# Feed-forward pairs, parts two and three: one product of 512 columns for both halves of an operand

## The chip, the cores and the metric

The kernel runs on one core of a Trainium2 chip. The metric is the device time of one execution in microseconds, as the median of several runs. A profile is the record of one such execution, taken by the hardware profiler. The engines are PE (the matrix engine TensorE; PEld is its weight loading), DVE (VectorE, element by element), ACT (ScalarE, copies and functions), POOL (GpSimd) and SP (SyncE, which issues transfers). Products are summed in PSUM, a small memory of eight banks, each of 512 fp32 numbers per partition; DVE and ACT read them out into SBUF, where all other tiles lie.

## The reference

The program is an encoder of two layers over 512 tokens of 1024 channels. Each layer mixes tokens by three parallel branches, then runs a gated feed-forward part and a gated input embedding. Only the feed-forward part is touched:

```python
D_FF = int(math.ceil(8 * D_MODEL / 3 / 256) * 256)   # 2816
...
h = rmsnorm(x, norm_ffn[i])
x = x + (jax.nn.silu(h @ w_ffn_gate[i]) * (h @ w_ffn_up[i])) @ w_ffn_down[i]
```

All arrays are fp32, the inputs x, p and the parameters are drawn from normal distributions, and the output is (1, 512, 1024).

## The kernel before, in words

**Precision.** PE multiplies operands of type fp32r, which keep fewer bits than fp32. So every operand is split into a high part (a rounded copy, made on ACT) and a low part (the rest, by a subtraction on DVE; `split`, line 162). A product is three matmuls added into one PSUM tile: high weight by high operand, high weight by low operand, low weight by high operand. `mm3` (lines 175 to 179) does this for most of the kernel, with 512 columns (tokens) each.

**The feed-forward part** (`ffn`, line 1094) has 22 blocks of 128 inner channels. They come in three parts of 8, 7 and 7 blocks (`PARTS`, line 40). In each part the blocks' gate and up products are made first (the *pair stage*; a *pair* is one block's gate and up weights), then the part's share of the down product is made for the eight output blocks and subtracted from x (the *down stage*).

**A pair** (`seven`, line 959) treats gate and up, and the two halves of the tokens and of the channels, as a 2 by 2 product of blocks, and makes it with seven products in place of eight (the Strassen-Winograd scheme). Weights are a11, a12, a22 and the sums s1 to s4; operands are b11, b21, b22 and the sums t1 to t4. Each product sums over four k-blocks of 128 channels and has 256 columns (half of the tokens): four times the three matmuls of lines 1004 to 1006, 84 matmuls for a pair. The operands are made once per layer in `quarters` (line 928): t1 to t4 are tiles of shape [128, 2, 256], high part and low part one behind the other; b11, b21 and b22 are cut out of the tiles h, [128, 2, 512], in which the high part's 512 columns lie ahead of the low part's.

**The running sums.** Partial sums live in the PSUM tiles C, A, Q (three banks, of the tags mm for even blocks and sc, sc, av for odd ones) and T (tag tr). They hold 256 columns each, half of a bank. In parts two and three the steps of a pair, each ended by a `yield`, are:

1. C = a11·b11; ACT copies C into A.
2. T = s1·t3; ACT copies T into uu[:, 0].
3. A += s3·t2; ACT copies A into Q; the gate of the pair before is started (`flush`: Silu on ACT, multiply on DVE, then the split into the down product's operand); C += a12·b21 (`corner`), and DVE writes C times the row factor rb into gg[:, 0].
4. A += s2·t1; ACT copies A into uu[:, 1]; Q += a22·t4; DVE adds uu[:, 0] to uu[:, 1] and Q to uu[:, 0].
5. A += s4·b22; DVE writes A times rb into gg[:, 1].

**The order of the work.** PE's order is the program's. `sevens_of` (line 1058) weaves two pairs: step 1 of the next, 4 of this one, 2 of the next, 5 of this one, 3 of the next; the last pair of a part runs its steps 4 and 5 alone. The other engines' orders are set by the compiler's scheduler from priorities; weight loading and splitting are put up to 400 instructions ahead (line 963). Each engine then works strictly through its own queue, waiting at an instruction until what that one needs is there. A pair's weights need, on ACT and DVE, two splits of 1024 columns (a11 with a12, s1 with s2), one of 512 (a22), two additions on DVE (s3, s4) and a third split of 1024 columns (s3 with s4, into tiles of tags pt or y). The sums s1 and s2 are formed by transfers that POOL issues (line 974).

The first block of part one has a variant of its own (`early`), which the change leaves as it is.

Of the kernel before, what the change touches and what calls it, by code (L numbers as in the profile page):

```python
# [12 lines left out]
F32R = mybir.dt.float32r  # L13
I32 = mybir.dt.int32
AF = mybir.ActivationFunctionType
ALU = mybir.AluOpType
# [4 lines left out]
P = 128  # L21
# [40 lines left out]
class Net:  # L62
# [211 lines left out]
    def norm_chunk(self, k, x, g, tag, st, n=512):  # L274

        if k == KD - 1:
            self.sumsq(k, x, st)
        if n < 512:
            tag = tuple(a[:, :n] for a in self.halves(self.sb(tag, [P, 2, 512], F32R)))
        h = self.operand(x[:, :n], g, tag)  # L280
        if k < KD - 1:
            self.sumsq(k, x, st)
        return h
# [644 lines left out]
    def quarters(self, x, h, j):  # L928


        one, two = slice(0, 256), slice(256, 512)
        g = lambda k: self.par(self.i, "ffn", k)
        f = []
        for k in (2 * j, 2 * j + 1):
            v = self.sb("t", [P, 512])
            self.act(v, x[k], AF.Copy, scale=g(k))
            f.append(v)
        b11, b12, b21, b22 = f[0][:, one], f[0][:, two], f[1][:, one], f[1][:, two]
        u = self.sb("t", [P, 2, 256])
        w = self.sb("t", [P, 2, 256])  # L940
        t1, t2, t3, t4 = u[:, 0], u[:, 1], w[:, 0], w[:, 1]
        self.tt(t1, b11, b12, ALU.subtract)
        self.stt(t2, t1, -1.0, b22, ALU.mult, ALU.subtract)
        self.tt(t3, b22, b12, ALU.subtract)
        self.stt(t4, t2, -1.0, b21, ALU.mult, ALU.subtract)
        if j < 2:
            d = [self.sb("rp", [P, 2, 256], F32R) for _ in range(2)]
            d += [self.sb("b", [P, 2, 256], F32R) for _ in range(2)] if j else \
                self.parts_of("v", [2, 256], 2, F32R)
        else:  # L950
            d = [q for n in range(2) for q in self.zs[2 * j - 4 + n]]
        for o, t in zip(d, (t1, t2, t3, t4)):
            self.held = self.split(o[:, 0], o[:, 1], t)
        ha, hb = self.halves(h[2 * j]), self.halves(h[2 * j + 1])
        cut = lambda p, c: (p[0][:, c], p[1][:, c])
        return dict(b11=cut(ha, one), b21=cut(hb, one), b22=cut(hb, two),
                    **{f"t{n + 1}": (o[:, 0], o[:, 1]) for n, o in enumerate(d)})

    def seven(self, wg, wu, bs, tags, spare, md, first, fb, early):


        nc = self.nc
        with self.tc.high_priority(offset=min(self.w_ahead, self.tc.cur_priority - self.p0)):
            lo, up = slice(0, 512), slice(512, 1024)
            g, a22 = self.sb("wr", [P, 1024]), self.sb("r", [P, 512])
            sums = self.sums[self.sevens % 3], self.sums[3]
            self.sevens += 1
            s1, s2, s3, s4 = (s[:, q:q + 512] for s in sums for q in (0, 512))
            nc.sync.dma_start(s1, wg[:, lo])
            nc.sync.dma_start(s2, wu[:, up])  # L970
            nc.sync.dma_start(g, wg)
            nc.sync.dma_start(a22, wu[:, up])
            for q in (s1, s2):
                nc.gpsimd.dma_start(q, wu[:, lo], accum_op=ALU.add)  # L974
            ws = {}

            def halve(hi, lo, src, names):
                i = self.split(hi, lo, src)
                for q, name in enumerate(names):
                    c = slice(q * 512, q * 512 + 512)  # L980
                    ws[name] = (hi[:, c], lo[:, c])
                return i

            wide = lambda: (self.sb("wh", [P, 1024], F32R), self.sb("wl", [P, 1024], F32R))
            i = halve(*wide(), g, ("a11", "a12"))
            if fb == 1:
                self.behind(i, self.held)
            low = halve(self.sb("kh", [P, 512], F32R), self.sb("a", [P, 512], F32R), a22, ("a22",))
            halve(*wide(), sums[0], ("s1", "s2"))
            i = self.tt(s3, s1, a22, ALU.add)  # L990
            self.behind(i, low)
            if first or fb < 3:
                self.behind(i, self.held if fb else self.mark)
            self.tt(s4, s3, g[:, up], ALU.add)
            halve(*spare, sums[1], ("s3", "s4"))
        C, A, Q = (self.ps(t, (P, 256)) for t in tags)

        def product(out, w, b, first=False):
            wh, wl = ws[w]
            mm = nc.tensor.matmul  # L1000
            for k in range(4):
                c = slice(k * P, k * P + P)
                bh, bl = bs[k][b]
                mm(out, wh[:, c], bh, start=first and k == 0, stop=False, skip_group_check=True)  # L1004
                mm(out, wh[:, c], bl, start=False, stop=False, skip_group_check=True)  # L1005
                mm(out, wl[:, c], bh, start=False, stop=k == 3, skip_group_check=True)  # L1006
            self.chunk2()

        gg, uu = self.sb("t", [P, 2, 256]), self.sb("t", [P, 2, 256])
        def corner():  # L1010
            product(C, "a12", "b21")
            if not early:
                self.tt(gg[:, 0], C, self.halved(0), ALU.mult)

        product(C, "a11", "b11", True)
        self.act(A, C, AF.Copy)
        yield
        if early:
            Z = self.ps("tr", (P, 256))
            product(Z, "s4", "b22", True)  # L1020
            self.act(gg[:, 1], Z, AF.Copy)
            corner()
            yield
        T = self.ps("tr", (P, 256))
        product(T, "s1", "t3", True)
        self.act(uu[:, 0], T, AF.Copy)
        yield
        product(A, "s3", "t2")
        self.flush(self.act(Q, A, AF.Copy))
        if not early:  # L1030
            corner()
        yield
        product(A, "s2", "t1")
        self.act(uu[:, 1], A, AF.Copy)
        product(Q, "a22", "t4")
        self.tt(uu[:, 1], uu[:, 1], uu[:, 0], ALU.add)
        self.tt(uu[:, 0], Q, uu[:, 0], ALU.add)
        if early:
            self.tt(gg[:, 0], C, self.halved(0), ALU.mult)
            self.tt(gg[:, 1], A, gg[:, 1], ALU.add)  # L1040
        yield
        if not early:
            product(A, "s4", "b22")
        self.tt(gg[:, 1], gg[:, 1] if early else A, self.halved(1), ALU.mult)

        def rest(then):
            i = self.act(gg, gg, AF.Silu, table="silu")
            if then is not None:
                self.behind(i, then)
            self.tt(gg, gg, uu, ALU.mult)  # L1050
            self.held = self.split(*self.halves(md), gg.rearrange("p a b -> p (a b)"))

        self.pending.append(rest)
# [40 lines left out]
    def ffn(self, h, x):  # L1094
# [3 lines left out]
        st, hn, bs = [], [], self.four  # L1098
# [4 lines left out]
        for part in PARTS:  # L1103
            mids = md8[:len(part)]
            self.sevens_of((self.seven(self.a["w_fg"][i, fb], self.a["w_fu"][i, fb], bs,
                                       (("mm", "mm", "mm"), ("sc", "sc", "av"))[fb % 2],
                                       spare[fb % 2], md8[f], part[0] and f < 2, fb, fb == 0)
                            for f, fb in enumerate(part)), part[0] == 0)
            self.flush()
            down = [self.a["w_fd"][i, m][:, part[0] * P:(part[-1] + 1) * P] for m in range(KD)]  # L1110
            two = [self.ps(("mm", "sc")[part[-1] % 2 == 0]) for _ in range(2)]
            self.pair(two, down[:2], mids)
            for m in range(KD):
                if m < 2:
                    ps = two[m]
                else:
                    ps = self.ps("mm")
                    self.gemm(ps, down[m], mids)
                d = self.sb("t", [P, 512])
                self.tt(d, ps, self.rb, ALU.mult)  # L1120
                self.tt(x[m], x[m], d, ALU.subtract)
                if part is PARTS[-1]:
                    if m in (0, 2):
                        qk = self.parts_of("qk", [2, 512], 2, F32R)
                    hn.append(self.norm_chunk(m, x[m], self.par(i, "ple", m),
                                              qk[m % 2] if m < 4 else "z", st))
# [350 lines left out]
```

## Time and profile before

| | |
|---|---|
| median of 3 runs | 1771.03 us (1770.5 to 1771.51) |
| the profiled execution | 1770.93 us |
| its span, first to last instruction | 1769.2 us |
| granted TensorE clock | 0.999 of full |
| pair stages of parts two and three, both layers | 617.2 to 687.6, 725.7 to 796.1, 1493.7 to 1564.1, 1602.2 to 1672.5 us |

The profile's page gives busy time per engine and, as its fourth part, the chain of work that ended last: followed back from the last instruction, at each step to what released it. The windows view gives, for a stretch of the span, its length and each engine's busy time in it, with the number of instructions in brackets. The timeline has one row for each instruction: its start, its duration, its engine, the line of the kernel that issued it, the tile written and the tiles read, the shape; in square brackets stands how long the engine was idle before it and what ended that. Lines 143 and 157 are the helpers through which nearly all of ACT's and DVE's work goes, so their rows are told apart by their tiles: ffn_wh and ffn_wl are high and low weights, ffn_wr, ffn_r and ffn_qk raw ones and their sums, ffn_t the gates' tiles uu and gg, ffn_mm, ffn_sc, ffn_av and ffn_tr PSUM tiles by tag, wo_rb the row factor.

A matmul's duration reaches from its start until its results are written; the next one starts long before that. What a matmul costs PE is therefore the time from its start to the next one's.

### The profile page before, as it was taken

How to read it: one execution, taken by the hardware profiler on the slowest of the kernel's cores; microseconds unless marked ns; L12 is line 12 of the kernel's file. 1: busy time of each engine (PE TensorE's matmuls, PEld its weight loads, DVE VectorE, ACT ScalarE, POOL GpSimd, SP SyncE). 2: the span in 40 equal slices, each digit the busy share in tenths (PEclk: the TensorE clock that was granted, in tenths of full speed). 3: DMA queues.
4: the chain of work that ended last, by engine and by line, in shares of the span. 5: the costliest groups of instructions: out<-in, count | busy, mean ns of one | idle time of the engine just before them, and what ended most of it. 6: DMA issues, size and time to landing. Idle time of an engine off the chain costs nothing.

```text
span 1769.2 us, 27111 instructions
## 1 busy us (share of the span) xinstructions
PE 1760.0 (99%) x10146; PEld 1553.3 (88%) x10146; DVE 1361.1 (77%) x2220; ACT 900.6 (51%) x1559; POOL 104.0 (6%) x114
## 2 busy tenths in 40 slices
PE   9999999999999999999999999999999999999998
PEld 7889888888899899998888888888888998989987
DVE  7967988998787576777776789789888865866676
ACT  5566555326575254454545655552356643634444
POOL 0000000000121010100000000000001210101000
PEclk9999999999999999999999999999999999999999
DMA  6575642334767375543546655323356664655332
GB/s 229 158 191 156 169 116 56 104 104 154 208 170 183 107 172 150 143 120 125 158 128 168 193 141 163 100 76 94 103 192 177 179 168 118 173 144 155 95 104 96
DMA packets 114788, 253.95 MB, mean 144 GB/s; under 512 B 16864, under 2 KB 23776, under 8 KB 114656
## 3 DMA queue, kind: packets, MB, share of 16 engines
q1 hardware_dynamic: 101264, 227.83, 42.5%
q0 software_dynamic: 12672, 23.07, 8.1%
q8 instruction: 80, 1.31, 0.3%
q10 hardware_dynamic: 720, 1.31, 0.2%
q14 instruction: 52, 0.43, 0.1%
HBM read 215.46 MB, written 7.34 MB: 126 GB/s over the span
## 4 chain that ended last, share of the span: by engine, by line
PE 98%; DVE 1%; ACT 1%; issue 0%; POOL 0%; POOLq 0%; ACTq 0%; DVEq 0%
PE ffn_mm L177 4%; PE ffn_mm L178 4%; PE ffn_mm L179 4%; PE ffn_mm L1006 3%; PE ffn_mm L1004 3%; PE ffn_mm L1005 3%; PE ffn_sc L1004 3%; PE ffn_sc L1005 3%; PE ffn_sc L1006 3%; PE mergea_mm L177 2%; PE mergea_mm L179 2%; PE mergea_mm L178 2%; PE diff_sc L796 2%; PE diff_mm L177 2%; PE diff_mm L178 2%; PE gatec_mm L178 2%
## 5 line engine op out<-in xcount | busy, mean ns | idle before, releaser
L160 DVE SCALAR_TENSOR_TENSOR conv_z<-glu_z,pre_par,conv_z 128x512 f32<-128x512 f32 x240 | 179.6, 748 | 3.4
L143 ACT ACTIVATE ffn_wh<-ffn_wr 128x1024 fp32r<-128x1024 f32 (+1 forms) x92 | 93.3, 1021 | 141.8 <-PE ffn_mm L178 76.6
L157 DVE TENSOR_TENSOR ffn_wl<-ffn_wr,ffn_wh 128x1024 fp32r<-128x1024 f32 (+1 forms) x92 | 107.6, 1175 | 41.3 <-ACT ffn_wh L143 40.9
L974 POOL DMA_DIRECT2D ffn_qk<-w_fu x88 | 77.9, 981 | 601.6 <-DMA ffn_qk<-w_fu 288.0
L157 DVE TENSOR_TENSOR ffn_t<-ffn_mm,wo_rb 128x512 f32<-128x512 f32 (+1 forms) x86 | 47.8, 557 | 72.2 <-PE ffn_mm L179 61.9
L143 ACT ACTIVATE mergea_wh<-mergea_wr 128x1024 fp32r<-128x1024 f32 (+1 forms) x32 | 27.1, 846 | 96.8 <-PE mergea_mm L178 79.6
L157 DVE TENSOR_TENSOR ffn_wl<-ffn_qk,ffn_wh 128x1024 fp32r<-128x1024 f32 x44 | 53.9, 1224 | 15.2 <-ACT ffn_wh L143 15.2
L143 ACT ACTIVATE ffn_wh<-ffn_qk 128x1024 fp32r<-128x1024 f32 x44 | 46.6, 1059 | 33.0 <-PE ffn_mm L178 16.2
L143 ACT ACTIVATE diff_a<-diff_sc,diff_s 128x512 f32<-128x512 f32 x32 | 22.0, 688 | 71.1 <-DVE diff_s L889 71.1
L177 PE MATMUL ffn_mm<-ffn_v,ffn_wh 128*128 128x512 f32 x132 | 51.4, 389 | 0.0
L178 PE MATMUL ffn_mm<-ffn_v,ffn_wh 128*128 128x512 f32 x132 | 51.4, 389 | 0.0
L179 PE MATMUL ffn_mm<-ffn_v,ffn_wl 128*128 128x512 f32 x132 | 51.3, 389 | 0.0
L177 PE MATMUL ffn_mm<-ffn_y,ffn_wh 128*128 128x512 f32 x132 | 51.3, 389 | 0.0
L178 PE MATMUL ffn_mm<-ffn_y,ffn_wh 128*128 128x512 f32 x132 | 51.3, 389 | 0.0
L179 PE MATMUL ffn_mm<-ffn_y,ffn_wl 128*128 128x512 f32 x132 | 51.3, 389 | 0.0
L1004 PE MATMUL ffn_mm<-wo_h,ffn_wh 128*128 128x256 f32 x176 | 49.9, 284 | 0.0
L1005 PE MATMUL ffn_sc<-wo_h,ffn_wh 128*128 128x256 f32 x176 | 49.8, 283 | 0.0
L1006 PE MATMUL ffn_mm<-wo_h,ffn_wl 128*128 128x256 f32 x176 | 49.8, 283 | 0.0
L1006 PE MATMUL ffn_sc<-wo_h,ffn_wl 128*128 128x256 f32 x176 | 49.8, 283 | 0.0
L1004 PE MATMUL ffn_sc<-wo_h,ffn_wh 128*128 128x256 f32 x176 | 49.8, 283 | 0.0
L1005 PE MATMUL ffn_mm<-wo_h,ffn_wh 128*128 128x256 f32 x176 | 49.8, 283 | 0.0
L143 ACT ACTIVATE natten_wh<-natten_wr 128x1024 fp32r<-128x1024 f32 x24 | 25.4, 1058 | 42.1 <-issue 15.2
(862 smaller groups left out, 6483.4 us busy)
## 6 DMA issues: line engine op xcount, KB each, us to landing
ffn_qk<-w_fu POOLq DMA_DIRECT2D x88, 256.0 KB, 6.4
ffn_wr<-w_fg SPq DMA_DIRECT2D x44, 512.0 KB, 4.4
ffn_wr<-w_fd SPq DMA_DIRECT2D x32, 448.0 KB, 4.2
ffn_r<-w_fu SPq DMA_DIRECT2D x44, 256.0 KB, 3.2
ffn_qk<-w_fg SPq DMA_DIRECT2D x44, 256.0 KB, 3.1
ffn_qk<-w_fu SPq DMA_DIRECT2D x44, 256.0 KB, 3.3
natten_wr<-w_in SPq DMA_DIRECT2D x16, 512.0 KB, 4.4
diff_wr<-w_in SPq DMA_DIRECT2D x16, 512.0 KB, 4.2
```

The lines of the kernel that those rows point to most:

```text
L143: i = self.nc.scalar.activation(out, in_, func, **kw)
L157: return self.nc.vector.tensor_tensor(out, a, b, op)
L160: return self.nc.vector.scalar_tensor_tensor(out, a, s, b, op0, op1)
L177: mm(out, wh, ah, start=first, stop=False, **kw)
L178: mm(out, wh, al, start=False, stop=False, **kw)
L179: mm(out, wl, ah, start=False, stop=last, **kw)
L796: self.nc.tensor.matmul(out, st4[:, u, qs], keys(st), start=first and n == 0, stop=n == 1, **kw)
L974: nc.gpsimd.dma_start(q, wu[:, lo], accum_op=ALU.add)
L1004: mm(out, wh[:, c], bh, start=first and k == 0, stop=False, skip_group_check=True)
L1005: mm(out, wh[:, c], bl, start=False, stop=False, skip_group_check=True)
L1006: mm(out, wl[:, c], bh, start=False, stop=k == 3, skip_group_check=True)
```

## The change

In parts two and three (`twice`), C, A and Q get 512 columns, in two halves of 256: a full bank. A product into such a tile makes, per k-block, one matmul of the high weights with the operand's high and low parts side by side (512 columns; the sums with the high part land in the first half, those with the low part in the second), and one of the low weights with the high part (256 columns, first half). So it has two matmuls where it had three. T keeps its 256 columns and its three matmuls. The two halves are added when a tile is read out. As one DVE instruction doesn't take both halves from PSUM here, ACT copies the second half to SBUF and DVE adds the first one to it. The copies of C into A and of A into Q take both halves. T goes to gg[:, 1] and is added to both parts of uu in one broadcast addition. C is read at the end of step 5 and no longer in step 3, and both parts of gg are multiplied by rb in one instruction. Operands are handed on as [128, 2, 256] slices in place of tuples of two; part one takes its three matmuls from these slices.

```diff
@@ norm_chunk
-            tag = tuple(a[:, :n] for a in self.halves(self.sb(tag, [P, 2, 512], F32R)))
+            tag = self.sb(tag, [P, 2, 512], F32R)[:, :, :n]
@@ quarters
-        ha, hb = self.halves(h[2 * j]), self.halves(h[2 * j + 1])
-        cut = lambda p, c: (p[0][:, c], p[1][:, c])
-        return dict(b11=cut(ha, one), b21=cut(hb, one), b22=cut(hb, two),
-                    **{f"t{n + 1}": (o[:, 0], o[:, 1]) for n, o in enumerate(d)})
+        ha, hb = h[2 * j], h[2 * j + 1]
+        return dict(b11=ha, b21=hb[:, :, one], b22=hb[:, :, two],
+                    **{f"t{n + 1}": o for n, o in enumerate(d)})
@@ seven
-        C, A, Q = (self.ps(t, (P, 256)) for t in tags)
+        shape = (P, 2, 256) if twice else (P, 256)
+        C, A, Q = (self.ps(t, shape) for t in tags)
...
-                bh, bl = bs[k][b]
-                mm(out, wh[:, c], bh, start=first and k == 0, stop=False, skip_group_check=True)
-                mm(out, wh[:, c], bl, start=False, stop=False, skip_group_check=True)
-                mm(out, wl[:, c], bh, start=False, stop=k == 3, skip_group_check=True)
+                both = bs[k][b]
+                if len(out.shape) > 2:
+                    mm(out, wh[:, c], both, start=first and k == 0, stop=False, skip_group_check=True)
+                    mm(out[:, 0], wl[:, c], both[:, 0], start=False, stop=k == 3, skip_group_check=True)
+                    continue
+                mm(out, wh[:, c], both[:, 0], start=first and k == 0, stop=False, skip_group_check=True)
+                mm(out, wh[:, c], both[:, 1], start=False, stop=False, skip_group_check=True)
+                mm(out, wl[:, c], both[:, 0], start=False, stop=k == 3, skip_group_check=True)
@@ corner
-            if not early:
+            if not early and not twice:
                 self.tt(gg[:, 0], C, self.halved(0), ALU.mult)
@@ step 2
-        self.act(uu[:, 0], T, AF.Copy)
+        shared = gg[:, 1] if twice else uu[:, 0]
+        self.act(shared, T, AF.Copy)
@@ step 4
         product(A, "s2", "t1")
-        self.act(uu[:, 1], A, AF.Copy)
+        if twice:
+            self.act(uu[:, 1], A[:, 0], AF.Copy)
+            self.act(gg[:, 0], A[:, 1], AF.Copy)
+        else:
+            self.act(uu[:, 1], A, AF.Copy)
         product(Q, "a22", "t4")
-        self.tt(uu[:, 1], uu[:, 1], uu[:, 0], ALU.add)
-        self.tt(uu[:, 0], Q, uu[:, 0], ALU.add)
+        if twice:
+            self.tt(uu[:, 1], uu[:, 1], gg[:, 0], ALU.add)
+            self.act(uu[:, 0], Q[:, 1], AF.Copy)
+            self.tt(uu[:, 0], Q[:, 0], uu[:, 0], ALU.add)
+            self.tt(uu, uu, gg[:, 1:2].to_broadcast([P, 2, 256]), ALU.add)
+        else:
+            self.tt(uu[:, 1], uu[:, 1], uu[:, 0], ALU.add)
+            self.tt(uu[:, 0], Q, uu[:, 0], ALU.add)
@@ step 5
-        self.tt(gg[:, 1], gg[:, 1] if early else A, self.halved(1), ALU.mult)
+        if twice:
+            for n, o in enumerate((C, A)):
+                self.act(gg[:, n], o[:, 1], AF.Copy)
+                self.tt(gg[:, n], o[:, 0], gg[:, n], ALU.add)
+            self.tt(gg, gg, self.rb.rearrange("p (a b) -> p a b", a=2), ALU.mult)
+        else:
+            self.tt(gg[:, 1], gg[:, 1] if early else A, self.halved(1), ALU.mult)
```

`ffn` passes `part[0] > 0` as `twice`.

More of the change, by code (lines that the diff above doesn't have):

```diff
@@ L953, in quarters, with seven @@
             self.held = self.split(o[:, 0], o[:, 1], t)
-        ha, hb = self.halves(h[2 * j]), self.halves(h[2 * j + 1])
-        cut = lambda p, c: (p[0][:, c], p[1][:, c])
-        return dict(b11=cut(ha, one), b21=cut(hb, one), b22=cut(hb, two),
-                    **{f"t{n + 1}": (o[:, 0], o[:, 1]) for n, o in enumerate(d)})
-    def seven(self, wg, wu, bs, tags, spare, md, first, fb, early):
+        ha, hb = h[2 * j], h[2 * j + 1]
+        return dict(b11=ha, b21=hb[:, :, one], b22=hb[:, :, two],
+                    **{f"t{n + 1}": o for n, o in enumerate(d)})
+    def seven(self, wg, wu, bs, tags, spare, md, first, fb, early, twice):
         nc = self.nc
@@ L1106, in ffn @@
                                        (("mm", "mm", "mm"), ("sc", "sc", "av"))[fb % 2],
-                                       spare[fb % 2], md8[f], part[0] and f < 2, fb, fb == 0)
+                                       spare[fb % 2], md8[f], part[0] and f < 2, fb, fb == 0,
+                                       part[0] > 0)
                             for f, fb in enumerate(part)), part[0] == 0)
```

## The prediction

> **What bounds the kernel now.** I read the page first (busy times and the chain that ended last), then the stages of the feed-forward part in the windows view, then the timeline of PE, ACT and DVE inside one of them.
>
> ```profile
> span 1769.2 us, 27111 instructions
> ...
> PE 1760.0 (99%) x10146; PEld 1553.3 (88%) x10146; DVE 1361.1 (77%) x2220; ACT 900.6 (51%) x1559; POOL 104.0 (6%) x114
> ...
> PE 98%; DVE 1%; ACT 1%; issue 0%; POOL 0%; POOLq 0%; ACTq 0%; DVEq 0%
> ```
>
> PE is busy nearly without a hole and makes up 98% of the chain that ended last. So time leaves this kernel only where PE gets shorter, and it comes back wherever another engine makes PE wait. The stages that the change touches are the pairs of parts two and three in both layers:
>
> ```profile
> core 0: us, PE busy (x) PEld busy (x) DVE busy (x) ACT busy (x) POOL busy (x), PEclk, DMA share, GB/s
> 617.20:687.60 70.40, 70.40 (x589) 70.33 (x589) 51.36 (x77) 41.00 (x67) 12.38 (x14) 1.00 0.69 169
> 687.60:725.70 38.10, 38.10 (x170) 31.54 (x169) 23.87 (x33) 10.18 (x11) 0.00 (x0) 1.00 0.37 117
> 725.70:796.10 70.40, 70.40 (x590) 70.36 (x589) 50.78 (x76) 39.74 (x65) 7.03 (x8) 1.00 0.52 136
> 1493.70:1564.10 70.40, 70.40 (x590) 70.36 (x589) 51.40 (x77) 40.99 (x67) 12.37 (x14) 1.00 0.69 170
> 1602.20:1672.50 70.30, 70.30 (x589) 70.27 (x588) 50.73 (x76) 39.73 (x65) 7.08 (x8) 1.00 0.49 128
> ```
>
> The four rows of about 70.4 us are the pair stages; the 38.1 us row is a down stage, shown for its matmuls of 512 columns. In each pair stage PE is busy from end to end at full clock. Seven pairs of 84 matmuls are 588 (the count takes in one or two that straddle an edge).
>
> **What a matmul costs here.** A start-to-start time is what a matmul adds to PE, since the durations overlap. From the windows: 70.35 us / 588 = 119.6 ns for 256 columns, and 38.1 us / 168 (eight outputs of seven blocks, three each) = 226.8 ns for 512. The single rows agree, at both changes of width:
>
> ```profile
> 573.58 0.28 PE L1006 MATMUL ffn_sc<-wo_h,ffn_y 128*128 128x256 f32 x1
> 573.70 0.40 PE L177 MATMUL ffn_mm<-ffn_v,ffn_wh 128*128 128x512 f32 x1
> 573.93 0.40 PE L178 MATMUL ffn_mm<-ffn_v,ffn_wh 128*128 128x512 f32 x1
> ...
> 617.02 0.39 PE L179 MATMUL ffn_mm<-ffn_e,ffn_wl 128*128 128x512 f32 x1
> 617.25 0.28 PE L1004 MATMUL ffn_mm<-wo_h,ffn_wh 128*128 128x256 f32 x1
> ```
>
> 256 before 512 takes 0.12 us, 512 before 256 takes 0.23, so a mixed order costs each its own time. Two of 256 are 239.2 ns, one of 512 is 226.8: each merged pair saves 12.4 ns.
>
> **Change, PE.** Six of a pair's seven products are merged; the seventh, into T (s1 by t3), is not, because T stays a tile of 256 columns and the new branch asks for three dimensions. A product has four k-blocks, so 6 x 4 = 24 merges in a pair, 24 x 7 x 4 stages = 672 in all: 672 x 12.4 ns = 8.4 us less PE. A pair goes from 10.05 us (70.35 / 7) to 9.75.
>
> The Trainium skill, page "TensorE: Matmul & The Clock Gate", section "Back-to-back issue gap", speaks against most of this: it puts the fixed cost of a warm matmul at about 2.5 ns over its columns, by which 672 merges are worth about 1.7 us (an estimate from that page). The rows disagree: 2 x 119.6 - 226.8 is 12.4 ns, and they decide.
>
> **Change, layout.** The sliced tiles in place of tuples (norm_chunk, quarters) name the same bytes with the same instructions: nothing. The moving operand b11, b21 or b22 now spans two runs of 256 columns that lie apart; no row of 512 columns has that. Bounds: nothing, and the whole 12.4 ns. I take nothing, nearest to the 512-column rows.
>
> **Change, ACT and DVE, in the middle of a stage.** Per pair ACT widens two copies (A from C, Q from A) to 512 and gains four of 256 (the second halves of A, Q, C and A again). DVE keeps its four ops of 256 and gains two of 512: the broadcast add of T, and one multiply by rb over both halves in place of a part of the old ones (the old multiplies become adds). The rows:
>
> ```profile
> 681.98 0.37 ACT L143 ACTIVATE ffn_mm<-ffn_mm 128x256 f32<-128x256 f32 x1 [2.49 <-PE ffn_mm L1006]
> 682.26 0.62 ACT L143 ACTIVATE ffn_t<-ffn_t 128x512 f32<-128x512 f32 x1
> ...
> 643.42 0.42 DVE L157 TENSOR_TENSOR ffn_t<-ffn_mm,wo_rb 128x256 f32<-128x256 f32 x1
> 644.28 1.23 DVE L157 TENSOR_TENSOR ffn_wl<-ffn_qk,ffn_wh 128x1024 fp32r<-128x1024 f32 x1 [0.45 <-ACT ffn_wh L143]
> 645.43 0.69 DVE L157 TENSOR_TENSOR ffn_v<-ffn_t,ffn_v 128x512 fp32r<-128x512 f32 x1
> 647.16 1.23 DVE L157 TENSOR_TENSOR ffn_wl<-ffn_wr,ffn_wh 128x1024 fp32r<-128x1024 f32 x1 [1.05 <-ACT ffn_wh L143]
> 648.31 0.68 DVE L157 TENSOR_TENSOR ffn_a<-ffn_r,ffn_kh 128x512 fp32r<-128x512 f32 x1
> 648.91 0.68 DVE L157 TENSOR_TENSOR ffn_qk<-ffn_qk,ffn_r 128x512 f32<-128x512 f32 x1
> 649.51 0.42 DVE L157 TENSOR_TENSOR ffn_t<-ffn_t 128x256 f32<-128x256 f32 x1
> 649.85 0.68 DVE L157 TENSOR_TENSOR ffn_qk<-ffn_qk,ffn_wr 128x512 f32<-128x512 f32 x1
> 650.45 0.42 DVE L157 TENSOR_TENSOR ffn_t<-ffn_mm,ffn_t 128x256 f32<-128x256 f32 x1
> 650.78 0.41 DVE L157 TENSOR_TENSOR ffn_t<-ffn_mm,wo_rb 128x256 f32<-128x256 f32 x1
> 651.71 1.22 DVE L157 TENSOR_TENSOR ffn_pt<-ffn_qk,ffn_pt 128x1024 fp32r<-128x1024 f32 x1 [0.52 <-ACT ffn_pt L143]
> 652.86 0.68 DVE L157 TENSOR_TENSOR ffn_t<-ffn_t,ffn_t 128x512 f32<-128x512 f32 x1
> 653.46 0.42 DVE L157 TENSOR_TENSOR ffn_t<-ffn_sc,wo_rb 128x256 f32<-128x256 f32 x1
> ```
>
> That is one whole DVE period, 643.42 to 653.46: 10.04 us, of which 0.45 + 1.05 + 0.52 = 2.02 waits on ACT. Work is thus 8.02 us. A row is followed 0.60 us later where it has 512 columns and 0.33 where it has 256, so the change adds 1.2: 9.22 us of work in 9.75. DVE goes from 80% to 95% of the period and keeps 0.53 us for waits. ACT works 41.00 / 7 = 5.9 us a pair; a copy of 256 is followed after 0.28 us and one of 512 should take about 0.26 more, so it gains 4 x 0.28 + 2 x 0.26 = 1.6 and has 7.5 of 9.75. Neither is over its limit by the sum. A further question is what each makes PE wait for. The closest is the buffer of C. Today the row at 643.42 reads C right after its last product and so frees it; changed, C is freed by an add in the pair's last step. PE wants that buffer two pairs on:
>
> ```profile
> 653.10 0.28 PE L1004 MATMUL ffn_mm<-wo_h,ffn_wh 128*128 128x256 f32 x1
> ```
>
> One period before it, at 643.06, the next pair's first product began. In the changed period that start falls to 643.06 + 9.75 = 652.81. On DVE the add of C comes, in program order, behind the row now at 649.85 and the two sums of Q and T: 650.45 + 0.33 + 0.60 + 0.42 = 651.80. That is 1.0 us in time, so I cost it at nothing; the cover is this 1.0 us, and the rival below is what happens when it is gone. The other new waits have more room: A's first half is accumulated on only two products (2.8 us) after its two copies can begin.
>
> **Change, at the end of a stage.** There nothing is interleaved: the last pair's s2 product is followed by one product of Q and then s4, which writes A and must wait for the copies of A. ACT takes the next weights' split first:
>
> ```profile
> 684.21 0.62 ACT L143 ACTIVATE ffn_y<-ffn_t 128x512 fp32r<-128x512 f32 x1
> 684.79 0.96 ACT L143 ACTIVATE ffn_wh<-ffn_wr 128x896 fp32r<-128x896 f32 x1
> 685.65 0.36 ACT L143 ACTIVATE ffn_t<-ffn_mm 128x256 f32<-128x256 f32 x1
> ...
> 685.97 0.28 PE L1006 MATMUL ffn_mm<-wo_z,ffn_a 128*128 128x256 f32 x1
> 686.09 0.37 PE L1004 MATMUL ffn_mm<-wo_h,ffn_pt 128*128 128x256 f32 x1
> ```
>
> The copy of A ends at 686.01 and s4 begins at 686.09, 0.08 us longer than its neighbours: it already just waits. One more copy before it is 0.28 us, and the two products ahead of it get 2 x 4 x 12.4 ns = 0.10 us shorter while ACT's chain does not: 0.38 us a stage, 1.5 us in four. Bounds: -0.3 us in all if ACT takes the copies before that split (the 0.08 goes as well), and about +4 if the second copy falls behind one more split of 512 (0.62 us). I take 1.5, as the present order has it. The end of the gating chain also grows, by a copy, an add and a wider multiply, about 1.2 us; the down product uses that operand last of its seven blocks, after 2 x 6 x 3 x 226.8 ns = 8.2 us, which hides it.
>
> **Sum.** -8.4 + 1.5 = -6.9 us. The profiled execution took 1770.93 us (its span and 1.7 around it), within 0.1 of the median of 1771.03; I go from the median: 1764.1 us.
>
> **Rivals.**
>
> (a) *DVE frees C too late, and the kernel is slower.* The split of s3 and s4 (the row at 651.71) belongs to the weights, which are put ahead of other work. If it stands before C's add in DVE's queue, the add follows it: 651.71 + 1.15 + 0.42 = 653.28, 0.47 us after PE wants the buffer at 652.81. The period is then 10.22 us, 0.17 above today's 10.05. Six full periods in each of four stages: 24 x 0.17 = 4.1 us, with 1.5 at the ends: 1776.7 us. It decides as soon as the add comes more than 1.0 us later than I put it. For it: only 0.53 us of DVE's period is left free, and the queue is in a fixed order. Against it: the split's high half needs ACT until 651.7, and the add can be ready 0.3 us sooner. Chance 0.18.
>
> (b) *Stalls of 0.1 to 0.3 us a pair,* the same mechanism half grown, eat 2.4 to 7 of the 8.4 us: 1766.5 to 1771. Chance 0.16, of which about half lies within 0.2% of the time before.
>
> (c) *The merge does not pay on PE*: a 512-column matmul with its halves apart, or next to one of 256, costs what two of 256 do, so PE saves nothing and the ends cost 4 x 0.28 = 1.1 us: 1772.1. For it, no row shows that operand; against it, the rows at 573.58 to 617.25. Chance 0.06. The Trainium skill, in the section of "TensorE: Matmul & The Clock Gate" named above, would leave 1.7 us of gain (its estimate) and so land near this case.
>
> **How the numbers follow.** My forecast, 1762 to 1766, has 0.60. A measurement can tell about 0.2%, or 3.5 us, from no change. Faster than 1767.5: the forecast and half of (b), 0.68. Within: the other half of (b), and (c), 0.14. Slower than 1774.6: (a), 0.18. The low end is 8.4 us plus the 0.3 of the ends, 1762.3, rounded to 1762; the high end 1774.5 takes in (b) and (c) and leaves out (a).
>
> **What would show it.** In the changed profile, right: 672 fewer matmuls (9474 in all); pair stages of about 68.6 us (70.35 - 2.1 + 0.4) each; one widened wait at the first s4 matmul of the last pair, ended by ACT; DVE busy around 60 us in each stage. Wrong: starts of more than 0.23 us at the merged lines would be (c); a wait at the first product of a pair (a11 by b11), ended by DVE, would be (a); stages as short as 68.2 us would say the end costs nothing.

## The result, and the profile after

| | before | changed |
|---|---|---|
| median | 1771.1 us (1770.2 to 1772.44, 13 runs) | 1774.64 us (1774.14 to 1776.15, 13 runs) |
| profiled execution | 1770.93 us | 1774.64 us |
| its span | 1769.2 us | 1772.9 us |

The ratio is 1.0021 (95% interval 1.0014 to 1.0028): about 3.5 us slower, where 7 us faster was forecast. The page of the changed kernel has these lines (span; busy time of each engine; the chain that ended last):

```profile
span 1772.9 us, 25953 instructions
...
PE 1758.6 (99%) x9474; PEld 1519.5 (86%) x9474; DVE 1396.6 (79%) x2276; ACT 943.8 (53%) x1671; POOL 103.9 (6%) x114
...
PE 92%; DVE 4%; ACT 2%; issue 1%; DMA 0%; POOL 0%; POOLq 0%; ACTq 0%; DVEq 0%
```

The 672 matmuls are gone (10146 - 9474). But PE now has 92% of the chain where it had 98%, and DVE has 4% where it had 1%: PE waits for somebody. The windows view of the four pair stages (length; busy time with instructions for PE, PEld, DVE, ACT and POOL; clock; DMA share; GB/s) says where:

```profile
617.81:689.27 71.46, 70.03 (x422) 61.72 (x421) 58.75 (x88) 50.82 (x93) 12.41 (x14) 1.00 0.68 167
727.35:798.39 71.04, 69.82 (x421) 61.53 (x420) 57.87 (x87) 50.22 (x92) 7.04 (x8) 1.00 0.52 135
1495.64:1567.10 71.46, 70.03 (x422) 61.72 (x420) 58.76 (x88) 50.82 (x93) 12.32 (x14) 1.00 0.69 168
1605.19:1676.23 71.04, 69.82 (x422) 61.55 (x420) 57.87 (x87) 50.21 (x92) 7.09 (x8) 1.00 0.50 127
```

Before, each stage took 70.35 us, all of it PE. Now they take 285.00 us together, 3.60 more than 4 x 70.35 = 281.40. So the whole slowdown lies in these stages, and each has 1.22 to 1.43 us in which PE is idle. The waits view of PE (engine, tile, line, what it waited for: us in total, times, longest) names two new ones:

```profile
PE ffn_sc L1005 <- DVE ffn_t L157: 4.6, 8, 0.6
...
PE ffn_mm L1005 <- ACT ffn_t L143: 0.5, 2, 0.3
```

The first one is the first product of an odd pair, a11 by b11, whose tile C has the tag sc. It waits for an addition on DVE. This is how it looks in PE's timeline:

```profile
643.19 0.28 PE L1006 MATMUL ffn_mm<-wo_h,ffn_wl 128*128 128x256 f32 x1
644.00 0.47 PE L1005 MATMUL ffn_sc<-wo_h,ffn_wh 128*128 128x512 f32 x1 [0.54 <-DVE ffn_t L157]
644.31 0.28 PE L1006 MATMUL ffn_sc<-wo_h,ffn_wl 128*128 128x256 f32 x1
```

A matmul normally starts 0.12 us after one of 256 columns. Here it starts 0.81 us after it, and the next comes 0.31 later where 0.23 is usual: 0.78 us lost. The idle time in brackets is less than the loss, since it counts from the modelled end of the matmul before. Taken from start to start, the eight waits cost 0.78 to 0.86 us each, 6.5 us in all.

DVE's timeline of the same time shows whom PE waits for:

```profile
640.30 0.69 DVE L157 TENSOR_TENSOR ffn_qk<-ffn_qk,ffn_wr 128x512 f32<-128x512 f32 x1
640.91 0.42 DVE L157 TENSOR_TENSOR ffn_t<-ffn_t,ffn_t 128x256 f32<-128x256 f32 x1
641.24 0.42 DVE L157 TENSOR_TENSOR ffn_t<-ffn_av,ffn_t 128x256 f32<-128x256 f32 x1
641.70 0.69 DVE L157 TENSOR_TENSOR ffn_t<-ffn_t,ffn_t 128x512 f32<-128x512 f32 x1
642.30 1.22 DVE L157 TENSOR_TENSOR ffn_y<-ffn_qk,ffn_y 128x1024 fp32r<-128x1024 f32 x1
643.44 0.75 DVE L157 TENSOR_TENSOR ffn_t<-ffn_sc,ffn_t 128x256 f32<-128x256 f32 x2
```

Read it by the tiles: the sum s4; the additions of uu, of Q (from the av tile) and of T; then the low split of s3 and s4, 1.22 us into ffn_y; and only then C out of the sc tile, in the last row (two additions, C's at 643.44 and A's behind it). C's addition ends at about 643.86 and PE starts at 644.00. ACT's timeline shows that it was a near thing:

```profile
641.09 1.06 ACT L143 ACTIVATE ffn_y<-ffn_qk 128x1024 fp32r<-128x1024 f32 x1 [1.51 <-DVE ffn_qk L157]
642.05 0.36 ACT L143 ACTIVATE ffn_t<-ffn_sc 128x256 f32<-128x256 f32 x1
```

The copy of C's second half, which the addition needs, is ready at about 642.4. DVE had gone into the split at 642.30, 0.1 us before. The copy was late because ACT took the high half of the same split first (641.09). At that time the copy could not start yet: by the program it writes gg[:, 0], and the addition at 640.91 reads A's second half out of there until 641.33. A tile of its own for this copy was not tried.

Even pairs have the same order on DVE and no such wait. DVE reads C of an even pair at 654.12, behind a split at 652.98, but PE had already begun the next even pair:

```profile
653.98 0.40 PE L1005 MATMUL ffn_mm<-wo_h,ffn_wh 128*128 128x512 f32 x1
```

That product would have written over sums still to be read, so C of the next even pair lies in another bank than this one. I infer that it is Q's, which is read in step 4. In an odd pair Q lies apart (av), and the next C gets the bank of the old C.

In the four stages ten odd pairs have an earlier odd pair in their own stage, and two of the ten do not wait. They are the first of that kind in part three of each layer, where DVE's queue has C's addition ahead of the split:

```profile
740.62 0.42 DVE L157 TENSOR_TENSOR ffn_t<-ffn_sc,ffn_t 128x256 f32<-128x256 f32 x1
741.56 1.23 DVE L157 TENSOR_TENSOR ffn_y<-ffn_qk,ffn_y 128x1024 fp32r<-128x1024 f32 x1
```

There PE starts the next odd pair at 742.90, 0.12 us after the row before.

The second new wait is the one at the end of a stage, forecast at 0.38 us. Here are ACT's and then PE's rows of the first stage's end:

```profile
686.21 0.94 ACT L143 ACTIVATE ffn_wh<-ffn_wr 128x896 fp32r<-128x896 f32 x1
687.05 0.64 ACT L143 ACTIVATE ffn_t<-ffn_mm 128x256 f32<-128x256 f32 x2
```

```profile
687.19 0.28 PE L1006 MATMUL ffn_mm<-wo_z,ffn_a 128*128 128x256 f32 x1
687.75 0.50 PE L1005 MATMUL ffn_mm<-wo_h,ffn_pt 128*128 128x512 f32 x1 [0.27 <-ACT ffn_t L143]
```

The two copies of A end at 687.69, behind the weights' split, and s4 by b22 starts at 687.75. Taken from start to start, this costs 0.55 us in part two and 0.33 in part three, 1.76 us in four stages.

Last, what PE gains. Three rows in steady running:

```profile
655.39 0.40 PE L1005 MATMUL ffn_sc<-wo_rp,ffn_wh 128*128 128x512 f32 x1
655.62 0.28 PE L1006 MATMUL ffn_sc<-wo_rp,ffn_wl 128*128 128x256 f32 x1
655.74 0.40 PE L1005 MATMUL ffn_sc<-wo_rp,ffn_wh 128*128 128x512 f32 x1
```

A block of 512 and 256 columns takes 0.35 us from start to start. The median over all is 350 ns (233 and 117), alike for operands whose halves touch and for those whose halves lie apart. Three of 256 took 3 x 119.6 = 358.8. So a merge saves 8.8 ns, and 672 of them 5.9 us.

The account is then: -5.9 (PE) + 6.5 (C) + 1.8 (ends of stages) = +2.4; of the +3.6 measured, 1.2 us is left. It is spread over starts that are a few hundredths late, such as three in the first stage (at 639.29, 649.97 and 670.58) that come 0.29 to 0.30 us after a 512-column row, where 0.23 is usual.

### The profile page after: what moved, and what is told of

It reads as the page before. It is cut to its first block, busy times and chain, and to the rows that moved or that the text cites. A ratio compares the mean times of both kernels' runs of the same rounds, so it can differ in the third digit from the quotient of the medians.

```text
span 1772.9 us, 25953 instructions
## 1 busy us (share of the span) xinstructions
PE 1758.6 (99%) x9474; PEld 1519.5 (86%) x9474; DVE 1396.6 (79%) x2276; ACT 943.8 (53%) x1671; POOL 103.9 (6%) x114
## 4 chain that ended last, share of the span: by engine, by line
PE 92%; DVE 4%; ACT 2%; issue 1%; DMA 0%; POOL 0%; POOLq 0%; ACTq 0%; DVEq 0%
PE ffn_mm L178 4%; PE ffn_mm L177 4%; PE ffn_mm L179 4%; PE ffn_mm L1005 3%; PE ffn_sc L1005 3%; PE mergea_mm L178 2%; PE mergea_mm L177 2%; PE mergea_mm L179 2%; PE diff_sc L796 2%; PE diff_mm L177 2%; PE diff_mm L178 2%; PE gatec_mm L178 2%; PE natten_mm L178 2%; PE gatec_mm L177 2%; PE gatec_mm L179 2%; PE diff_mm L179 2%
## 5 line engine op out<-in xcount | busy, mean ns | idle before, releaser
L157 DVE TENSOR_TENSOR ffn_t<-ffn_mm,wo_rb 128x512 f32<-128x512 f32 (+1 forms) x58 | 36.2, 624 | 58.7 <-PE ffn_mm L179 57.6
L157 DVE TENSOR_TENSOR ffn_t<-ffn_t,ffn_t 128x512 f32<-128x512 f32 (+1 forms) x100 | 61.4, 614 | 14.1 <-ACT ffn_t L143 13.4
L1005 PE MATMUL ffn_sc<-wo_h,ffn_wh 128*128 128x512 f32 x112 | 41.2, 402 | 4.6 <-DVE ffn_t L157 4.6
L889 DVE TENSOR_REDUCE diff_s<-diff_sc 128x1 f32<-128x512 f32 x64 | 42.2, 684 | 2.2 <-PE diff_sc L796 2.2
L223 POOL TENSOR_TENSOR diff_rc<-diff_sm,pre_power 128x4 f32<-128x4 f32 x8 | 8.9, 1116 | 561.1 <-DVE diff_sm L160 502.6
L143 ACT ACTIVATE natten_b<-natten_b,natten_s 128x256 f32<-128x256 f32 x64 | 30.4, 500 | 20.4 <-DVE natten_s L715 20.3
L1005 PE MATMUL ffn_mm<-wo_h,ffn_wh 128*128 128x512 f32 x112 | 40.6, 397 | 0.0
```

Source lines behind the costliest of these rows:

```text
L143: i = self.nc.scalar.activation(out, in_, func, **kw)
L157: return self.nc.vector.tensor_tensor(out, a, b, op)
L223: nc.gpsimd.tensor_tensor(col, ms, self.power, ALU.pow)
L889: nc.vector.tensor_reduce(out=m[:, u:u + 1], in_=sc, op=ALU.max, axis=AX.X, negate=True)
L1005: mm(out, wh[:, c], both, start=first and k == 0, stop=False, skip_group_check=True)
```

## The experiments

**The theories.** The first: the merge pays on PE, and a wait of another engine's making takes its place. C's addition stands behind the s3/s4 split on DVE, and an odd pair's C must have that bank. Its rival: the gain was small because the matmul of 512 columns or the fuller ACT and DVE cost PE time by themselves, so that moving the bank or the addition would only move the wait. The runs stand beside runs of the kernel before at 1771.1 to 1771.2 us (the single one without low weights beside one of 1771.85); "stages" are the four pair stages, 281.40 us before and 285.00 changed.

### Another bank for C

In odd pairs A and Q change places. Q then shares a tag with C, as in even pairs. The instructions and their order stay.

```diff
-                                       (("mm", "mm", "mm"), ("sc", "sc", "av"))[fb % 2],
+                                       (("mm", "mm", "mm"), ("sc", "av", "sc"))[fb % 2],
```

> One line against the changed kernel: in odd pairs C, A and Q take PSUM tiles of the tags sc, av, sc in place of sc, sc, av. Every engine's instructions keep their order; only the bank that the pair two later gets for C is another (the one that Q frees in step 4, as in the even pairs, in place of C's own, freed by the add in step 5). Theory 1, the bank of C is handed on too late: the waits at the first product of a pair (ffn_sc, two per stage, 0.70 to 0.78 us each and 0.08 after it, 6.5 us in all) go, and nothing else moves: 1774.6 - 6.5 = about 1768.2. Theory 2, DVE at its limit sets the pace of the pair and the bank is only where it shows: the waits come back at another product, 1774 to 1775.

Measured: 1768.97 us (11 runs), ratio 0.9987 (0.9978 to 0.9996). Stages 278.2 us. DVE still has the addition behind the split, at the same times as above:

```profile
642.30 1.22 DVE L157 TENSOR_TENSOR ffn_y<-ffn_qk,ffn_y 128x1024 fp32r<-128x1024 f32 x1
643.44 0.42 DVE L157 TENSOR_TENSOR ffn_t<-ffn_sc,ffn_t 128x256 f32<-128x256 f32 x1
```

But PE no longer waits for it:

```profile
643.18 0.28 PE L1006 MATMUL ffn_mm<-wo_h,ffn_wl 128*128 128x256 f32 x1
643.30 0.40 PE L1005 MATMUL ffn_sc<-wo_h,ffn_wh 128*128 128x512 f32 x1
```

The odd pair's first product starts 0.12 us after the row before, 0.14 us ahead of DVE's reading of the old C. The stages are 6.8 us shorter, about the 6.5 of the eight waits. So the late addition costs time only through the bank.

### C's addition ahead of the split

The other cure for the same wait: the bank stays, and the s3/s4 split is put behind C's addition of the pair two before.

```diff
-            halve(*spare, sums[1], ("s3", "s4"))
+            i = halve(*spare, sums[1], ("s3", "s4"))
+            if twice and fb % 2 in self.added:
+                self.behind(i, self.added[fb % 2])
...
-                self.tt(gg[:, n], o[:, 0], gg[:, n], ALU.add)
+                i = self.tt(gg[:, n], o[:, 0], gg[:, n], ALU.add)
+                if n == 0:
+                    self.added[fb % 2] = i
...
```

> Against the changed kernel only an order is added: DVE's half of the split of s3 and s4 is put behind the add that frees C of the pair whose weight tiles it takes over. Theory 1, DVE's queue order (the split ahead of the add) holds C: the add ends 1.1 us sooner, which is more than the wait of 0.7 to 0.8, so the eight waits go and the time is about 1768.2, as with other banks. Theory 2, DVE at its limit: DVE's work is the same, so the wait only moves and the time stays at 1774 to 1775.

Measured: 1768.64 us (11 runs), ratio 0.9985 (0.9976 to 0.9994). Stages 277.74 us. DVE and PE now:

```profile
641.45 0.42 DVE L157 TENSOR_TENSOR ffn_t<-ffn_sc,ffn_t 128x256 f32<-128x256 f32 x1
641.79 1.22 DVE L157 TENSOR_TENSOR ffn_y<-ffn_qk,ffn_y 128x1024 fp32r<-128x1024 f32 x1
```

```profile
642.11 0.28 PE L1008 MATMUL ffn_mm<-wo_h,ffn_wl 128*128 128x256 f32 x1
642.23 0.39 PE L1007 MATMUL ffn_sc<-wo_h,ffn_wh 128*128 128x512 f32 x1
```

C is read at 641.45, the split follows, and the first product starts 0.12 us after the row before it. Bank and order were each needed for the wait, and taking away either removes it.

### The matmuls of one width together

Each product makes its four matmuls of 512 columns first and then its four of 256. In the changed kernel a block of 512 and 256 columns takes 350 ns, 3.6 more than 226.8 + 119.6. This asks whether the change of width from one matmul to the next costs them.

```diff
+            cut = lambda k: slice(k * P, k * P + P)
+            if len(out.shape) > 2:
+                for k in range(4):
+                    mm(out, wh[:, cut(k)], bs[k][b], start=first and k == 0, stop=False, skip_group_check=True)
+                for k in range(4):
+                    mm(out[:, 0], wl[:, cut(k)], bs[k][b][:, 0], start=False, stop=k == 3, skip_group_check=True)
+                self.chunk2()
+                return
...
-                if len(out.shape) > 2:
-                    mm(out, wh[:, c], both, start=first and k == 0, stop=False, skip_group_check=True)
-                    mm(out[:, 0], wl[:, c], both[:, 0], start=False, stop=k == 3, skip_group_check=True)
-                    continue
```

> Against the changed kernel a product makes its four matmuls of 512 columns first and its four of 256 behind them, in place of taking turns. In the changed kernel a block of 512 and 256 takes 350 ns, where 226.8 + 119.6 = 346.4 were expected. Theory A, the change of width at each matmul costs about 1.8 ns: a product falls by 3 x 3.6 = 11 ns, 168 products by 1.8 us, of which the waits for C take some back: about 1773. Theory B, a matmul of these products costs 1.8 ns more whatever stands next to it: 1774.6.

Measured: 1769.28 us (11 runs), ratio 0.9989 (0.998 to 0.9998). That is lower than expected, because the order does more than expected. Stages 279.65 us, 5.35 shorter than in the changed kernel. The wait for C shrank, though nothing was done to it:

```profile
PE ffn_sc L1004 <- DVE ffn_t L157: 2.3, 8, 0.3
```

From start to start it is 0.53 us in place of about 0.8, so some 2.3 us less in eight; the ends of the stages, 0.69 us in place of 1.76, give 1.07. Likely reason, argued from the rows and not tried: PE is done with the high weights sooner, ACT's next weight split can take that tile sooner, and DVE's chain behind it starts sooner. The other 2 us are the small late starts and PE itself. PE's rows, of the first product of a stage up to the start of the next, and then the same for one in the middle, where a row holds two matmuls:

```profile
617.83 1.07 PE L1004 MATMUL ffn_mm<-wo_h,ffn_wh 128*128 128x512 f32 x4
618.73 0.64 PE L1006 MATMUL ffn_mm<-wo_h,ffn_wl 128*128 128x256 f32 x4
619.21 0.28 PE L1012 MATMUL ffn_tr<-wo_v,ffn_wh 128*128 128x256 f32 x1
...
630.45 0.62 PE L1004 MATMUL ffn_sc<-wo_rp,ffn_y 128*128 128x512 f32 x2
630.91 0.62 PE L1004 MATMUL ffn_sc<-wo_z,ffn_y 128*128 128x512 f32 x2
631.37 0.40 PE L1006 MATMUL ffn_sc<-wo_rp,ffn_y 128*128 128x256 f32 x2
631.61 0.40 PE L1006 MATMUL ffn_sc<-wo_z,ffn_y 128*128 128x256 f32 x2
631.85 0.39 PE L1004 MATMUL ffn_sc<-wo_h,ffn_wh 128*128 128x512 f32 x1
```

From 617.83 to 619.21 the first product takes 1.38 us, which is 4 x (226.8 + 119.6) = 1.386, the forecast's price. From 630.45 to 631.85 the later one takes 1.40 us. So the price per matmul held for the first product of a stage, and a later one costs some 0.02 us more.

### The sums in two halves, without the merge

As in the changed kernel, but the matmul of 512 columns is cut into two of 256, one into each half. This is what the reading out costs by itself.

```diff
-                    mm(out, wh[:, c], both, start=first and k == 0, stop=False, skip_group_check=True)
+                    mm(out[:, 0], wh[:, c], both[:, 0], start=first and k == 0, stop=False, skip_group_check=True)
+                    mm(out[:, 1], wh[:, c], both[:, 1], start=False, stop=False, skip_group_check=True)
```

> The changed kernel with its way of reading the sums out, but the matmul of 512 columns cut back into two of 256, one into each half of the bank: the evacuation alone. Theory 1, late bank: pairs take 10.05 us on PE again, so C's bank is wanted some 0.2 to 0.3 us later and each of the eight waits falls to about 0.5 us: 1771.1 + 8 x 0.5 + 1.5 at the ends of the stages = about 1776.5. Theory 2, DVE sets the pace: the pair stages stay as long as in the changed kernel, 1774.6.

Measured: 1778.13 us (5 runs), ratio 1.0036 (1.0024 to 1.0049), above both expectations. Stages 287.82 us:

```profile
PE ffn_sc L1005 <- DVE ffn_t L157: 3.0, 8, 0.4
```

From start to start this wait is 0.63 us, eight times 5.1; the ends of the stages are 1.4. Together that is the 6.4 us by which these stages are longer than before. The merge, between this kernel and the changed one, is worth 2.8 us: its 5.9 on PE, less 1.4 and 0.4 by which both waits get longer, less the 1.2 us of late starts. A faster PE reaches the bank sooner and then waits longer. The slower one here was expected to wait about 0.5 us, and waits 0.63: that is 1.0 us in eight, most of the miss.

### The copies of A ahead of the next weights

At the end of a stage ACT takes the copies of A before the high split of the second down weights.

```diff
+        self.copied = None
...
     def split(self, hi, lo, src):
-        self.act(hi, src, AF.Copy)
+        self.high = self.act(hi, src, AF.Copy)
...
-        ws = [self.weights(ap, n * P) for ap in aps]
+        ws = []
+        for m, ap in enumerate(aps):
+            ws.append(self.weights(ap, n * P))
+            if m and self.copied is not None:
+                self.behind(self.high, self.copied)
...
-            self.act(gg[:, 0], A[:, 1], AF.Copy)
+            self.copied = self.act(gg[:, 0], A[:, 1], AF.Copy)
...
             self.pair(two, down[:2], mids)
+            self.copied = None
```

> Against the changed kernel only an order is added: ACT's split of the down stage's second weights is put behind the two copies of A in the last pair's step 4. Theory 1, the last pair's s4 product waits for these copies because that split of 0.95 us stands ahead of them: its waits (0.43 and 0.11 us in part two, 0.22 and 0.11 in part three, 1.75 us over four stages) go, the eight waits for C stay: about 1772.9. Theory 2, the copies are late for another reason (DVE or the sums themselves): 1774.6.

Measured: 1772.75 us (11 runs), ratio 1.0010 (1.0001 to 1.0019). Stages 283.13 us, 1.87 less. ACT's rows, then PE's:

```profile
685.95 0.64 ACT L144 ACTIVATE ffn_t<-ffn_mm 128x256 f32<-128x256 f32 x2
686.48 1.79 ACT L144 ACTIVATE ffn_wh<-ffn_wr 128x896 fp32r<-128x896 f32 x2
```

```profile
686.91 0.28 PE L1011 MATMUL ffn_mm<-wo_z,ffn_a 128*128 128x256 f32 x1
687.03 0.40 PE L1010 MATMUL ffn_mm<-wo_h,ffn_pt 128*128 128x512 f32 x1
```

The copies are over at 686.59, and s4 follows the row before it in 0.12 us. The wait for C stays as it was (4.6 us in eight, in the waits view). So this second wait is a matter of ACT's order, independent of the first, and worth its 1.8 us.

### The cures together

C's addition ahead of the split, the widths together, and the copies of A first:

> Against the changed kernel three edits together: DVE's order of e2_order, the grouped matmuls of e3_grouped, ACT's order of e5_tail. If the waits for C, the change of width and the copies at a stage's end are separate costs that add up, no wait is left in the pair stages: seven pairs of one unmerged product (1.425 us) and six merged ones (1.400) are 68.8 us, four stages 275.1 where they were 281.4 before the change: 1771.2 - 6.3 = about 1764.9. If they overlap or a further limit of DVE lies just behind them: 1766 to 1768.

Measured: 1764.76 us (5 runs), ratio 0.9963 (0.995 to 0.9976). All four stages take 68.69 us, and PE is busy from end to end in each. The first:

```profile
617.95:686.64 68.69, 68.69 (x422) 61.42 (x421) 57.51 (x87) 49.77 (x92) 12.38 (x14) 1.00 0.71 170
```

The forecast had 68.6. Against before that is 6.64 us in all, 9.9 ns a merge. With A and Q changing places as well:

> As e6_order_grouped_tail, with the banks of e1_tags as well. If handing on the bank of C sooner and freeing it sooner are two cures for the same wait, the second adds nothing: within 0.5 us of e6_order_grouped_tail, about 1764.9. If each left a part of the wait: lower by more than 1 us.

Measured: 1764.72 us (5 runs), ratio 0.9964 (0.995 to 0.9978), stages 68.69 us each. The two cures for C's wait don't add up, which fits one and the same wait.

### Without the low weights

What makes a product in the middle of a stage 0.02 us longer than the first? DVE's own traffic was one guess. This kernel is the last one, without DVE's low splits; the low weights of a11, a12 and s1 to s4 are left out in parts two and three, so the matmuls read the high weights there. With DVE's part of the s3/s4 split gone, nothing is put behind C's addition.

```diff
-                i = self.split(hi, lo, src)
+                if lo is None:
+                    i, lo = self.act(hi, src, AF.Copy), hi
+                else:
+                    i = self.split(hi, lo, src)
...
-            wide = lambda: (self.sb("wh", [P, 1024], F32R), self.sb("wl", [P, 1024], F32R))
+            wide = lambda: (self.sb("wh", [P, 1024], F32R), None if twice else self.sb("wl", [P, 1024], F32R))
...
-            halve(*spare, sums[1], ("s3", "s4"))
+            halve(spare[0], None if twice else spare[1], sums[1], ("s3", "s4"))
```

> As e7_all, but in parts two and three the low weights of a11, a12 and s1 to s4 are left out: DVE's three subtractions of 1024 columns per pair are gone, and the low-weight matmuls take the high weights again (same number and shape of matmuls). DVE falls from about 9.2 to 5.7 us of work per pair. A merged product in the middle of a stage takes 1.400 us, the very first one of a stage 1.379. Theory A, PE is slowed by DVE's traffic: products fall toward 1.38, a stage from 68.69 to 68.1 us or less. Theory B, DVE has no part in it: 68.6 to 68.7 us.

Measured, in one run, 1763.97 us, beside one of 1771.85 before. The first stage, with all cures and then without the low splits as well:

```profile
617.40:686.09 68.69, 68.69 (x422) 61.40 (x420) 57.51 (x87) 49.77 (x92) 12.39 (x14) 1.00 0.70 170
```

```profile
617.16:685.85 68.69, 68.69 (x422) 61.41 (x421) 38.76 (x70) 50.29 (x92) 11.63 (x14) 1.00 0.69 169
```

DVE's busy time falls from 57.51 to 38.76 us, and the stage takes the same 68.69. So these splits are not what makes the products longer; the rest of DVE's work wasn't taken away.

### Part one as well

All cures, and the merge also in part one, but for its first block:

```diff
-                                       part[0] > 0)
+                                       fb > 0)
```

> As e7_all, with the merged products in part one too, from its second pair on (14 more pairs, 84 more merged products of about 1.40 us in place of 1.425). If PE is all that counts there as well: 84 x 0.025 = 2.1 us under e7_all, about 1762.8. If the evacuation meets part one's own work on ACT and DVE (operands made and split for the first pairs): no gain or a loss, 1765 to 1770.

Measured: 1761.89 us (5 runs), ratio 0.9946 (0.9933 to 0.9959): 9.2 us less than before, and the best of all here. Part one's pair stage, which had 73.62 us with the cures alone:

```profile
500.19:572.05 71.86, 71.24 (x439) 63.20 (x438) 62.80 (x96) 55.34 (x100) 12.37 (x14) 1.00 0.74 184
```

PE is idle for 0.62 us of its 71.86, while the stages of parts two and three stay at 68.69.

## Why the prediction was wrong

**The step that failed** is the middle of a stage: "That is 1.0 us in time, so I cost it at nothing; the cover is this 1.0 us". It cost 6.5 us. The working took the addition of C to come right behind the sums of Q and T in DVE's queue. In the trace of after the s3/s4 split stands between them, 1.14 us to the next start, and the 1.0 us is gone. The two runs that cure this, by the bank and by the order, bring the stages to 278.2 and 277.74 us, below the 281.40 of before. The row of that split stood in the prediction, directly behind the rows the sum was made of. The sum went by the order of the program, where the queue goes by the scheduler's.

Even in the order of the sum the cover would have been smaller. With the split put behind it, C's addition ends at 641.45 + 0.42 = 641.87 and PE starts at 642.23: 0.36 us of cover, not 1.0. The sum had left out A's addition, which comes between s4 and Q's (0.34 us), and that C's addition waits for ACT's copy.

**Rival (a)** named this mechanism, with the split as its cause, and its total of 1776.7 is 2 us above the measured time. Its price was put together differently: 24 periods with 0.17 us net each, where the trace has 8 waits of about 0.8. It took every pair to get the bank of the C two before it, and that holds for odd pairs only. That rival's reason against, that the addition could be ready 0.3 us sooner than the split, did not hold: C's copy, behind the split's own high half on ACT, was ready 0.1 us after DVE had taken the split.

**The PE term** was mis-sized: 12.4 ns a merge, measured 8.8 in the changed order and 9.9 with the widths together, so 5.9 us for 8.4. The number of merges and the price of the operand with its halves apart (nothing) were right. The price of a matmul from one width's rows holds for the first product of a stage and not for the later ones. The formula for isolated matmuls in the Trainium skill, page "TensorE: Matmul & The Clock Gate", section "Back-to-back issue gap", would have made a merge worth 2.5 ns. The trace disagrees, with 8.8 and 9.9 ns.

**The ends of the stages**: forecast 1.5 us, measured 1.76, and the run that puts the copies of A first took 1.87 off. Right, with the cause and the place named. DVE at about 60 us busy a stage was right as well (57.9 to 58.8), and so was the tail of the gating chain costing nothing: no wait of the down products was new in the waits view.

With every wait cured, the kernel takes 1764.8 us, near the forecast of 1764.1. That is no merit of the sum: its ends of stages are then at nothing (1.5 us) and its PE term is 1.8 us too large, so the two cancel.

## What to carry to other kernels

Where PE is busy from end to end, a saving on PE counts only as far as those who free its banks keep pace, so follow each bank to its next user and ask which instruction on another engine frees it, and what stands ahead of that one in the queue as scheduled, not as the program has it. An engine with slack can still be late for one instruction: DVE was busy for 58.75 of a stage's 71.46 us and kept PE waiting 0.8 us at a time. When such a wait shows, there are two places to mend: the order on the engine that frees the bank, and which tile shares a tag with which.

## What the runs showed of the hardware beyond what was expected

A product of four matmuls of 512 columns and four of 256 took 1.38 us as the first of a stage and 1.40 later on, at a granted clock of 1.00 in both. The 1.40 is the same for operands whose halves touch and for those whose halves lie apart, and the same with DVE busy for 57.51 or 38.76 us of the stage. What makes the difference of some 0.02 us a product stays open; ACT's traffic wasn't tried. In the kernel before, too, the price is not one of width alone: products of the same twelve matmuls of 256 columns take from 1.42 us (s1 by t3) to 1.44 (a11 by b11) in steady running, so 119.6 ns is a mean over them.
